# Expert blocks that skip empty places, and scan outputs made one head at a time

## The chip, the core and the metric

One Trainium2 chip, one of its cores. The metric is device time in microseconds from the first to the last instruction of one execution. The engines are TensorE (PE in the rows, its weight load PEld), VectorE (DVE), ScalarE (ACT), GpSimd (POOL) and SyncE (SP), which only issues DMAs here. 16 DMA engines move the data between HBM and SBUF for all of them.

## The reference

Two layers over 768 tokens of width 1024: 256 of a context and 512 latent ones. Layer 0 works on all 768, layer 1 updates the 512 latent ones alone. A layer has two halves.

The token mixer projects the tokens and sends them through a gated convolution and, beside it, through a recurrent scan in two directions with 8 heads of 64 channels. With a state S of 64 x 64 for each head and direction, one step is

```
sa = S kk;   S = S * decay - sa b^T + v k^T;   y = S r
```

The mixture of experts chooses for each token one of 4 groups and 2 of its 8 experts, so that 2 of 32 experts work on each token:

```
for expert e:  yb = (silu(xb @ w1[e]) * (xb @ w3[e])) @ w2[e]      # xb: the tokens of e
out[token] = sum over its two experts of gate * yb[its place]
```

Layer 0 thus fills 768 x 2 = 1536 places, layer 1 512 x 2 = 1024. A final RMSNorm closes the trunk. All data are float32.

## The kernel before

The two layers run one after the other, and a layer has four stages: the dense input products with the preparation of the scan (`stage_dense`), the scan itself (`stage_scan`), the output products and the router (`stage_out`, `route`), and the experts with the combination of their rows (`moe`, `combine`). A planner orders the instructions of each engine by its own model of their costs. Where the code says `manual_schedule`, the named engines keep the order in which the code issues; TensorE does so from `stage_dense` through the scan.

**Scan.** The tokens are cut into 12 chunks of 64. Heads are taken two at a time, a pair filling 128 partitions, and two pairs with both directions go together (`a` = 0, 1). `step` is one chunk: it forms right-hand sides from the state, multiplies them with inverted triangular matrices, updates the state (`St`, a block diagonal matrix of 128 x 128 for a pair, one 64 x 64 block for each head) and then makes the outputs, lines 966 to 983. The outputs of a chunk go into one PSUM tile `py`. For each of the four (pair, direction) groups, line 972 multiplies the state with the queries, all 128 columns of the state at once. It is left out in the first chunk, whose state is zero. Line 974 then adds, for each head apart, the product of its values with the masked scores. Layer 1 makes outputs from chunk 4 on only. The masks and the inverses of the next six chunks are made ahead in `inverses`: a substitution of 31 pairs of VectorE operations (lines 840 and 842), transposes (844, 846), then products on TensorE (864 and 874). Dense products of the convolution and the gates (`fillers`, line 331) stand between the steps, a fixed number after each part of a step. Their weights come through `weights` (line 222: load `wr`, three buffers; lines 312 and 313 split it into two parts). A float32 product shows as two records in the profile.

**Zeroing.** `bufY` in HBM has a row for each place: 32 experts of 64 places (`CAP`), then 24 overflow blocks of 64. `zero_rows` (line 162) clears the overflow rows in 12 writes of 512 KB on SP, each the repetition of a zeroed tile of 128 columns. They are issued one after another by the fillers of layer 0; the planner moved them up to the start of the first dense stage.

**Experts.** `route_ordered` gives every token a place in each of its two experts, and makes `slot`: for each place the number of its token, by a product of one-hot matrices with the token numbers `tok` (lines 1283 to 1292). A place without a token gets 0. The filled places of an expert are its first ones. `block` (line 1379) handles one expert: `gather` (line 1372) fetches the 64 rows of its places from `h2rows` with an indirect DMA on GpSimd into `xe` (two buffers); TensorE transposes them (line 1387); the products with w1, w3 and w2 follow (line 1399), six loads of 1 MB a block from SP through rings of 16 buffers (`er`, `ez`, `ex`, line 1136); and line 1421 stores the 64 result rows to their rows of `bufY`, a plain DMA on GpSimd. A block holds 72 matmuls. An expert with more than 64 tokens has overflow blocks; layer 0 runs one of them always and more in a loop if needed, layer 1 only in the loop. In this run there are 33 blocks in layer 0 and 32 in layer 1. `combine` fetches for each token its two rows of `bufY` (line 1459) and sums them with the gates.

Of the kernel before, what the change touches and what calls it, by code (L numbers as in the profile page):

```python
# [12 lines left out]
I32 = mybir.dt.int32  # L13
# [35 lines left out]
NOV = 24  # L49
DEC = math.exp(-0.5) / 2.0  # L50
NEG = -1.0e30

W_IN_ORDER = ([24, 25, 26] + [b + p for p in range(4) for b in (12, 16, 20)]
              + [b + j for j in range(4) for b in (4, 8, 0)]
# [11 lines left out]
CO = {}  # L66
_o = 0
for _n, _w in (("ident", 128), ("mask", 128), ("bones", 128), ("bmean", 128), ("ones", 128), ("ii", 64), ("tri", 128),
               ("i64", 64), ("sel", 2), ("i8", 8), ("i4", 4), ("i24", 24), ("i64k", 12), ("tok", 6)):
    CO[_n] = slice(_o, _o + _w)  # L70
    _o += _w
NCO = _o
# [2 lines left out]
def constants():  # L75
    c = np.zeros((P, NCO), np.float32)
    p = np.arange(P)[:, None]
    q = np.arange(P)[None, :]
    c[:, CO["ident"]] = p == q
    s = p % C  # L80
    t = q % C
    c[:, CO["mask"]] = np.where(q < C, s < t, s <= t)
    c[:, CO["bones"]] = (p // 64) == (q // 64)
    c[:, CO["bmean"]] = ((p // 64) == (q // 64)) * (-1.0 / 64)
    c[:, CO["ones"]] = 1.0
    c[:, CO["ii"]] = (p % 64) == np.arange(64)[None, :]
    c[:, CO["tri"]] = p < q
    c[:, CO["sel"]] = (p % 32) == np.arange(2)[None, :]
    c[:, CO["i64"]] = np.arange(64)
    c[:, CO["tok"]] = p + P * np.arange(6)  # L90
    c[:, CO["i8"]] = np.arange(8)
    c[:, CO["i4"]] = np.arange(4)
    c[:, CO["i24"]] = np.arange(24)
    c[:, CO["i64k"]] = 64.0 * (1 + np.arange(12))
    m = np.zeros((P, T + 1024), np.float32)
    m[:, :T] = (np.arange(T) % C) != 0
    m[:, T:] = np.eye(32, dtype=np.float32).reshape(1, 1024)
    return c, m
# [16 lines left out]
class Trunk:  # L115
# [46 lines left out]
    def zero_rows(self, pool):  # L162

        nc = self.nc
        z = self.sb(pool, [P, 128], "zrow")
        nc.gpsimd.memset(z, 0.0)
        v = self.bufY[NE * CAP:].rearrange("(p r) d -> p (r d)", p=P)
        n = v.shape[1]
        for i in range(0, n, 1024):
            nc.sync.dma_start(v[:, i:i + 1024].rearrange("p (a d) -> p a d", d=128),  # L170
                              rap(z[:], 0, [[0, 8], [1, 128]]))
            yield


# [736 lines left out]
    def step(self, a, i, AMs, Rf, RR, VU, KTr, nxt):  # L911


        nc, sp, k = self.nc, self.sp, self.k
        hq = [slice(h * 64, h * 64 + 64) for h in range(2)]
        prs = range(2)
        AM, ui = AMs[i % H], 4 * (i % H)
        if i == 0:
            self.Yt[a] = self.sb(sp, [P, 2, T], "Y")
            for j in range(2):  # L920
                s = self.St[a, j] = self.sb(sp, [P, 2, 2, P], f"St{j}")
                nc.gpsimd.memset(s, 0.0)
        Y = self.Yt[a]
        S = self.St[a, i % 2]
        if 0 < i < NCK - 1:
            S0 = self.sb(sp, [P, 2, 2, C], "S0", bufs=2)
            for q in hq:
                nc.gpsimd.tensor_tensor(S0[q], S[q, :, :, q],
                                        self.PC[q, 2 * a:2 * a + 2, :, i - 1:i].to_broadcast([C, 2, 2, C]), op=ALU.mult)
        ps = self.psum("pc", [P, 2, P], 2)  # L930
        for pr in prs:
            for d in range(2):
                ur = slice(64 - 64 * d, 128 - 64 * d)
                if i:
                    nc.tensor.matmul(ps[ur, pr], RR[:, pr, d, :C], S[:, pr, d, :], start=True, stop=False)
            for h, q in enumerate(hq):
                for d in range(2):
                    ur = slice(64 - 64 * d, 128 - 64 * d)
                    nc.tensor.matmul(ps[ur, pr, q], AM[:, d, pr, h, :C], VU[:, d, pr, q], start=i == 0,
                                     stop=i == 0 or h == 1)  # L940
        W = self.sb(sp, [P, 2, P], "W")
        nc.scalar.activation(W, ps, AF.Copy)
        yield 2
        ps = self.psum("pc", [P, 2, P], 2)
        for pr in prs:
            for h, q in enumerate(hq):
                for d in range(2):
                    ur = slice(64 - 64 * d, 128 - 64 * d)
                    nc.tensor.matmul(ps[ur, pr, q], Rf[ur, ui + 2 * pr + h, :], W[ur, pr, q], start=True, stop=True)
        nc.vector.tensor_copy(VU[64:128, 0], ps[64:128])  # L950
        nc.scalar.activation(VU[0:64, 1], ps[0:64], AF.Copy)
        yield 2
        if i < NCK - 1:
            ps = self.psum("pc", [P, 2, 2, C], 2)
            for pr in prs:
                for d in range(2):
                    for h, q in enumerate(hq):
                        nc.tensor.matmul(ps[q, pr, d, :], KTr[:, pr, d, q], VU[:, d, pr, q], start=True, stop=True)
            Sn = self.St[a, (i + 1) % 2]
            for q in hq:  # L960
                if i:
                    nc.vector.tensor_tensor(Sn[q, :, :, q], ps[q], S0[q], op=ALU.add)
                else:
                    nc.vector.tensor_copy(Sn[q, :, :, q], ps[q])
            yield 1
        yield from nxt
        if i >= self.c0:
            ps = self.psum("py", [P, 2, 2, C])
            for pr in prs:
                for d in range(2):  # L970
                    if i:
                        nc.tensor.matmul(ps[:, pr, d, :], S[:, pr, d, :], RR[:, pr, d, C:], start=True, stop=False)
                    for h, q in enumerate(hq):
                        nc.tensor.matmul(ps[q, pr, d, :], VU[:, d, pr, q], AM[:, d, pr, h, C:], start=i == 0, stop=True)

            m = CCK - 1 - i if i < CCK else NCK - 1 + CCK - i
            yf = Y[:, :, i * C:(i + 1) * C]
            yr = rap(Y[:], m * C + C - 1, [[T, 2], [-1, C]])
            for y, q in ((yf, ps[:, :, 0, :]), (yr, ps[:, :, 1, :])):
                if i < m:  # L980
                    nc.scalar.activation(y, q, AF.Copy)
                else:
                    nc.vector.tensor_tensor(y, y, q, op=ALU.add)
        yield 2
# [164 lines left out]
    def moe(self):  # L1149
# [5 lines left out]
        self.gathered = []  # L1155
        with tc.manual_schedule(engines={mybir.EngineType.Pool}):
            for e in range(2):
                self.gathered.append(self.gather(self.slot[:, e:e + 1]))
        self.prefetch(RING[l][2])
        for e in range(NE):  # L1160
            self.block(self.slot[:, e:e + 1], self.bufY[e * CAP:(e + 1) * CAP, :],
                       t["w1"][l, e], t["w3"][l, e], t["w2"][l, e])
            if e == 0:
                self.route_rest()
        n = 1 if self.full else 0
        for i in range(n):
            e = nc.values_load(self.ovt[0:1, i:i + 1], engines=[mybir.EngineType.SP], min_val=0, max_val=NE - 1)
            self.block(self.slot_over[:, i:i + 1], self.bufY[(NE + i) * CAP:(NE + i + 1) * CAP, :],
                       *self.chosen(e))
        self.overflow(n)  # L1170
        self.bp.release()
        self.ep2.release()
# [33 lines left out]
    def route_ordered(self):  # L1206
# [82 lines left out]
        count = self.sb(mp, [P, NE], "count")  # L1289
        V.tensor_copy(count, ps[:, nt, :])  # L1290
        self.slot = self.sb(mp, [CAP, NE], "slot", I32)
        V.tensor_copy(self.slot, pt)
        self.places = count, pos, oh2, ex

    def route_rest(self):

# [55 lines left out]
        for i in range(2 * nt):  # L1352
            self.nc.tensor.matmul(ps, Q[:, i, :], B[:, i, :], start=i == 0, stop=i == 2 * nt - 1)
        self.slot_over = self.sb(mp, [CAP, NOV], "slotv", I32)
        V.tensor_copy(self.slot_over, ps)
        pg = s_([nt], "pg")
        V.reduce_sum(pg, self.gexp, axis=AX.X)
        V.reciprocal(pg, pg)
# [10 lines left out]
        V.tensor_scalar(self.ovt[:, :NOV], ove, float(NE - 1), None, op0=ALU.min)  # L1369
        V.tensor_scalar(self.ovt[:, NOV:], ic[:, NE - 1:NE], 1.0 if self.full else 0.0, None, op0=ALU.max)  # L1370

    def gather(self, slot):

        xe = self.sb(self.bp, [CAP, D], "xe", bufs=2)
        self.nc.gpsimd.indirect_dma_start(out=xe[:], out_offset=None, in_=self.h2[:],  # L1375
                                          in_offset=bass.IndirectOffsetOnAxis(ap=slot, axis=0))
        return xe

    def block(self, slot, ydst, w1, w3, w2):

# [35 lines left out]
        yo = self.sb(self.bp, [P, D], "yo", bufs=2)[:CAP, :]  # L1418
        nc.scalar.activation(yo, py[CAP:], AF.Copy)  # L1419
        nc.vector.tensor_tensor(yo, py[:CAP], yo, op=ALU.add)  # L1420
        nc.gpsimd.dma_start(ydst, yo)

    def chosen(self, e):
        t, l = self.t, self.l
# [2 lines left out]
    def overflow(self, n0):  # L1427
# [2 lines left out]
        n = nc.values_load(self.ovt[0:1, NOV:NOV + 1], min_val=n0, max_val=NOV)  # L1430
        with tc.For_i(n0, n, 1) as i:
            e = nc.values_load(self.ovt[0:1, bass.ds(i, 1)], engines=[mybir.EngineType.SP], min_val=0, max_val=NE - 1)
            r = i * CAP + NE * CAP
            slot = self.sb(self.mp, [CAP, 1], "slot1", I32, bufs=1)
            nc.sync.dma_start(slot, self.slot_over[:, bass.ds(i, 1)])
            self.block(slot[:], self.bufY[bass.ds(r, CAP), :], *self.chosen(e))

    def combine(self):

# [119 lines left out]
```

## Time and profile before

| | |
|---|---|
| runs, us | 2964.94, 2961.85, 2952.41; median 2961.85 |
| profiled execution, us | 2971.3; span of its instructions 2969.3 |
| mean granted TensorE clock in it | 0.929 of full |
| busy share of the span | TensorE 87%, VectorE 42%, ScalarE 28%, GpSimd 14% |
| DMA | 741.84 MB, 250 GB/s over the span |

The stages of the profiled execution follow from the starts of their instructions: the first scan from about 365 to 840 us, the experts of layer 0 from about 1000 to 1555 us, the second scan from about 1935 to 2255 us, the experts of layer 1 from about 2383 to 2925 us.

In the rows, an engine's busy time counts its instructions' spans; several can overlap. A window's row gives, for PE, PEld, DVE, ACT and POOL in this order, busy us and the number of instructions, then the granted clock as a share of full, the share of the DMA engines' time and what they moved. In a timeline, the brackets at the end hold the idle time before and what ended it.

### The profile page before, as it was taken

The page shows a single profiled execution, that of the slowest core. Times are in us where ns is not written, and L with a number is a line of the kernel's source. Part 1 is how long each engine was busy: PE and PEld are TensorE (multiplying, and loading weights), DVE is VectorE, ACT ScalarE, POOL GpSimd, SP SyncE. Part 2 cuts the span into 40 slices and gives each one's busy share as a digit, 9 for nine tenths or more (in the row PEclk, how much of TensorE's full clock was granted, in tenths as well). Part 3 has the DMA queues.
Part 4 walks back from the last instruction along what each step waited for, and adds up shares of the span by engine and source line. Part 5 has one row for each costly group of instructions (what it writes and reads, how often), then busy time and mean ns, then how long its engine had stood idle before and what let it go on. Part 6 is the DMA issues. An engine that isn't in the chain of part 4 may idle for free. (4 is left out here: it accounts for less than half of the span.)

```text
span 2969.3 us, 44287 instructions
## 1 busy us (share of the span) xinstructions
PE 2571.9 (87%) x17505; PEld 1677.7 (57%) x17505; DVE 1237.5 (42%) x2618; ACT 838.4 (28%) x1603; POOL 422.9 (14%) x554
## 2 busy tenths in 40 slices
PE   6998899999989699888887997898998779888886
PEld 4676677777778443333337774566666634333334
DVE  4686553736463411111115786546646421111113
ACT  4453333333222111111112552443442211111111
POOL 0232011111130200000001231111211110000001
PEclk9999899998989799999998998888999989999998
DMA  7457445552554899999974467554446699999994
GB/s 277 138 164 228 147 159 166 166 183 84 170 179 150 319 403 393 398 398 392 398 311 169 119 188 243 188 167 132 144 127 187 233 345 391 391 397 400 390 404 157
DMA packets 284833, 741.84 MB, mean 250 GB/s; under 512 B 53712, under 2 KB 138960, under 8 KB 228560
## 3 DMA queue, kind: packets, MB, share of 16 engines
q1 hardware_dynamic: 271344, 694.42, 65.1%
q0 software_dynamic: 13280, 44.57, 4.5%
q8 instruction: 139, 2.28, 0.3%
q14 instruction: 70, 0.57, 0.1%
HBM read 647.41 MB, written 91.49 MB: 249 GB/s over the span
## 5 line engine op out<-in xcount | busy, mean ns | idle before, releaser
L331 PE MATMUL pd<-hh,wh 128*128 128x512 f32 (+1 forms) x912 | 352.4, 426 | 11.7 <-ACT hh L312 3.8
L331 PE MATMUL pd<-hh,wl 128*128 128x512 f32 (+1 forms) x912 | 311.7, 382 | 10.3 <-DVE wl L313 10.3
L331 PE MATMUL pd<-hl,wh 128*128 128x512 f32 (+1 forms) x912 | 311.7, 382 | 1.1 <-DVE hl L313 1.1
L1399 PE MATMUL pd<-ez,xs 128*64 128x512 f32 x1024 | 257.4, 635 | 37.6 <-DMA ez<-in_w 27.0
L313 DVE TENSOR_TENSOR wl<-wr,wh 128x512 fp32r<-128x512 f32 x236 | 166.2, 705 | 245.0 <-ACT wh L312 244.0
L1408 DVE COPY hs<-pd 128x512 f32<-128x512 f32 x65 | 45.0, 692 | 525.1 <-PE pd L1399 525.1
L312 ACT ACTIVATE wh<-wr 128x512 fp32r<-128x512 f32 x236 | 148.6, 631 | 321.3 <-PE pd L331 217.1
L331 PEld LDWEIGHTS pd<-hh,wh 128*128 128x128 f32 x912 | 163.5, 197 | 92.6 <-issue 30.1
L1399 PE MATMUL pd<-er,xs 128*64 128x512 f32 x672 | 172.9, 635 | 22.8 <-DMA er<-in_w 15.0
L331 PEld LDWEIGHTS pd<-hh,wl 128*128 128x128 f32 x912 | 163.7, 198 | 46.7 <-DVE wl L313 13.6
L1412 PEld LDWEIGHTS pt<-cst,hs 128*128 128x128 f32 x1040 | 125.6, 192 | 111.8 <-issue 56.0
L1420 DVE TENSOR_TENSOR yo<-py,yo 64x1024 f32<-64x1024 f32 x65 | 79.1, 1217 | 252.4 <-ACT yo L1419 239.4
L331 PEld LDWEIGHTS pd<-hl,wh 128*128 128x128 f32 x912 | 164.5, 198 | 29.5 <-DVE hl L313 2.3
L1399 PEld LDWEIGHTS pd<-ez,xs 128*64 128x64 f32 x1024 | 78.2, 144 | 178.2 <-issue 127.3
L1412 PE MATMUL pt<-cst,hs 128*128 128x64 f32 x1040 | 142.2, 281 | 26.5 <-DVE hs L1408 17.3
L1375 POOL DMA_INDIRECT xe<-h2rows,slot x64 | 60.0, 937 | 624.0 <-PE px L1387 595.4
L1399 PE MATMUL py<-ez,hid 128*64 128x512 f32 x520 | 127.7, 627 | 8.7 <-DVE yo L1420 7.8
L1389 ACT ACTIVATE xs<-px 128x512 f32<-128x512 f32 x65 | 38.8, 598 | 293.4 <-PE px L1387 287.6
L1399 PE MATMUL pd<-ex,xs 128*64 128x512 f32 x384 | 99.9, 644 | 21.7 <-DMA ex<-in_w 16.7
L1414 ACT ACTIVATE hid<-pt 128x256 f32<-128x256 f32 x65 | 25.0, 384 | 327.9 <-PE pt L1412 325.8
L1399 PEld LDWEIGHTS pd<-er,xs 128*64 128x64 f32 x672 | 48.9, 143 | 112.9 <-issue 83.6
L1410 ACT ACTIVATE hs<-pd 128x512 f32<-128x512 f32 x65 | 38.8, 597 | 240.9 <-PE pd L1399 240.8
(378 smaller groups left out, 4539.7 us busy)
## 6 DMA issues: line engine op xcount, KB each, us to landing
ez<-in_w SPq DMA_DIRECT2D x193, 1024.0 KB, 22.2
er<-in_w SPq DMA_DIRECT2D x125, 1024.0 KB, 22.3
ex<-in_w SPq DMA_DIRECT2D x72, 1024.0 KB, 22.3
wm<-in_w_mod SPq DMA_DIRECT2D x48, 1024.0 KB, 6.4
wr<-in_w_in SPq DMA_DIRECT2D x172, 256.0 KB, 3.1
bufY<-yo POOLq DMA_DIRECT2D x65, 256.0 KB
dKB<-KB SPq DMA_DIRECT2D x16, 768.0 KB, 5.2
dRR<-RR SPq DMA_DIRECT2D x16, 768.0 KB, 4.6
```

What stands on the lines that cost most here:

```text
L312: self.nc.scalar.activation(hi, src, AF.Copy)
L313: self.nc.vector.tensor_tensor(lo, src, hi, op=ALU.subtract)
L331: nc.tensor.matmul(p, a[:, k], h[:, kt, s], start=kt == 0 and j == 0, stop=kt == nk - 1 and j == 2)
L1375: self.nc.gpsimd.indirect_dma_start(out=xe[:], out_offset=None, in_=self.h2[:], in_offset=bass.IndirectOffsetOnAxis(ap=slot, axis=0))
L1389: nc.scalar.activation(xs, ps, AF.Copy)
L1399: nc.tensor.matmul(out[h * CAP:(h + 1) * CAP, c:c + 512], a[:, kt, :], w[:, i + h, c:c + 512], start=kt < 2, stop=kt >= nk - 2)
L1408: nc.vector.tensor_copy(hs, ps)
L1410: nc.scalar.activation(hs, ps, AF.Copy)
L1412: nc.tensor.matmul(pt[:, i, c, :], hs[:, c * P:(c + 1) * P], k["ii"], start=True, stop=True)
L1414: nc.scalar.activation(hid, pt[:, 0], AF.Silu)
L1420: nc.vector.tensor_tensor(yo, py[:CAP], yo, op=ALU.add)
```

## The change

Four edits go together.

Places without a token: `tok` holds the token number less `FAR` = 8192, and 8192 is added again when `slot` is made. A filled place has its token as before; an empty one has 8192. The gather gets a bound of 767 and drops places above it. The two buffers of `xe` are cleared before their first use.

Stores: `rows_of` makes `dst`, the row of `bufY` of each place, with 8192 added where the place is empty. The plain store becomes an indirect one over the whole of `bufY`, with its last row as the bound. The loop over further overflow blocks fetches its column of `dst` too.

Zeroing: `zero_rows` clears all 3584 rows instead of the 1536 of the overflow, in 28 writes of 512 KB, from a tile of 256 columns.

Scan outputs: the product with the state is made for each head apart, with the 64 columns of that head.

```diff
-    c[:, CO["tok"]] = p + P * np.arange(6)
+    c[:, CO["tok"]] = p + P * np.arange(6) - FAR
+    c[:, CO["row"]] = p + CAP * np.arange(NE + NOV)
...
-        z = self.sb(pool, [P, 128], "zrow")
+        z = self.sb(pool, [P, 256], "zrow")
         nc.gpsimd.memset(z, 0.0)
-        v = self.bufY[NE * CAP:].rearrange("(p r) d -> p (r d)", p=P)
+        v = self.bufY[:].rearrange("(p r) d -> p (r d)", p=P)
         n = v.shape[1]
         for i in range(0, n, 1024):
-            nc.sync.dma_start(v[:, i:i + 1024].rearrange("p (a d) -> p a d", d=128),
-                              rap(z[:], 0, [[0, 8], [1, 128]]))
+            nc.sync.dma_start(v[:, i:i + 1024].rearrange("p (a d) -> p a d", d=256),
+                              rap(z[:], 0, [[0, 4], [1, 256]]))
...
-                        nc.tensor.matmul(ps[:, pr, d, :], S[:, pr, d, :], RR[:, pr, d, C:], start=True, stop=False)
+                        for q in hq:
+                            nc.tensor.matmul(ps[q, pr, d, :], S[:, pr, d, q], RR[:, pr, d, C:], start=True, stop=False)
...
-                self.gathered.append(self.gather(self.slot[:, e:e + 1]))
+                self.gathered.append(self.gather(self.slot[:, e:e + 1], True))
...
-            self.block(self.slot[:, e:e + 1], self.bufY[e * CAP:(e + 1) * CAP, :],
+            self.block(self.slot[:, e:e + 1], lambda: self.dst[:, e:e + 1],
...
-        V.tensor_copy(self.slot, pt)
+        V.tensor_scalar(self.slot, pt, float(FAR), None, op0=ALU.add)
+        self.dst = self.sb(mp, [CAP, NE + NOV], "dst", I32)
+        self.rows_of(0, NE, self.slot)
...
+    def rows_of(self, a, b, slot):
+        V = self.nc.vector
+        V.tensor_scalar(self.dst[:, a:b], slot, float(FAR), float(FAR), op0=ALU.is_ge, op1=ALU.mult)
+        V.tensor_tensor(self.dst[:, a:b], self.dst[:, a:b], self.k["row"][:CAP, a:b], op=ALU.add)
...
-        V.tensor_copy(self.slot_over, ps)
+        V.tensor_scalar(self.slot_over, ps, float(FAR), None, op0=ALU.add)
+        self.rows_of(NE, NE + NOV, self.slot_over)
...
-    def gather(self, slot):
+    def gather(self, slot, first=False):
         xe = self.sb(self.bp, [CAP, D], "xe", bufs=2)
+        if first:
+            self.nc.gpsimd.memset(xe, 0.0)
         self.nc.gpsimd.indirect_dma_start(out=xe[:], out_offset=None, in_=self.h2[:],
-                                          in_offset=bass.IndirectOffsetOnAxis(ap=slot, axis=0))
+                                          in_offset=bass.IndirectOffsetOnAxis(ap=slot, axis=0),
+                                          bounds_check=T - 1, oob_is_err=False)
...
-        nc.gpsimd.dma_start(ydst, yo)
+        nc.gpsimd.indirect_dma_start(out=self.bufY[:], out_offset=bass.IndirectOffsetOnAxis(ap=dst(), axis=0), in_=yo,
+                                     in_offset=None, bounds_check=(NE + NOV) * CAP - 1, oob_is_err=False)
```

## Rows read from the trace of the kernel before

**Rows 1.** the page, share of DMA by slice, and its software queue

```profile
DMA  7457445552554899999974467554446699999994
q0 software_dynamic: 13280, 44.57, 4.5%
```

**Rows 2.** windows, experts of layer 1; columns: busy us (count) by engine, clock, DMA share, GB/s

```profile
2460.00:2520.00 60.00, 58.46 (x304) 25.06 (x302) 9.13 (x12) 9.80 (x15) 4.96 (x7) 1.00 1.02 391
```

**Rows 3.** waits of SP, experts of layer 0; columns: total us, times, longest

```profile
SPq L1136 <- DMA ez<-in_w: 164.4, 66, 4.2
```

**Rows 4.** windows over the two scans

```profile
365.00:840.00 475.00, 440.51 (x4264) 348.55 (x4263) 237.81 (x628) 151.27 (x343) 74.32 (x126) 0.95 0.50 157
1935.00:2255.00 320.00, 291.81 (x2947) 215.53 (x2945) 180.65 (x455) 118.69 (x265) 54.91 (x93) 0.93 0.47 143
```

**Rows 5.** DMA queues, 1100 to 1500 us; columns: packets, MB, share of 16 engines

```profile
q1 hardware_dynamic: 20050, 146.03, 92.1%
```

**Rows 6.** a window in which GpSimd issues nothing

```profile
1490.00:1500.00 10.00, 9.21 (x46) 3.92 (x42) 0.69 (x1) 0.00 (x0) 0.00 (x0) 1.00 1.02 422
```

**Rows 7.** GpSimd's groups; columns: busy us, mean ns, idle before

```profile
L1375 POOL DMA_INDIRECT xe<-h2rows,slot x64 | 60.0, 937 | 624.0 <-PE px L1387 595.4 <-DMA h2rows<-hr 9.2 <-DMA xe<-h2rows,slot 7.7
...
L1421 POOL DMA_DIRECT2D bufY<-yo x65 | 34.8, 535 | 375.2 <-DVE yo L1420 349.4 <-DVEq L1431 25.8
...
L922 POOL MEMSET St<- 128x512 f32 x8 | 4.1, 525 | 31.4 <-PE py L972 26.2 <-issue 5.3
```

**Rows 8.** waits of GpSimd, experts of layer 0

```profile
POOL xe L1375 <- PE px L1387: 263.5, 23, 16.9
```

**Rows 9.** timeline of GpSimd, start of the experts; columns: start us, us

```profile
999.18 1.14 POOL L1375 DMA_INDIRECT xe<-h2rows,slot  x1 [3.99 <-DVE slot L1292]
```

**Rows 10.** timeline of TensorE, one output block of the scan

```profile
509.94 0.33 PE L972 MATMUL py<-RRs,St 128*128 128x64 f32 x2
510.20 0.34 PE L974 MATMUL py<-AM,VU 128*64 128x64 f32 x4
...
512.35 0.49 PE L250 MATMUL pd<-cst,mrow 128*128 128x2 f32 x3
```

**Rows 11.** timeline of TensorE, the first chunk's output block

```profile
368.97 0.69 PE L974 MATMUL py<-AM,VU 128*64 128x64 f32 x16
369.59 0.62 PE L331 MATMUL pd<-hh,wh 128*128 128x512 f32 x2
```

**Rows 12.** the product with S, whole run; columns: ns min/median/max, first and last start

```profile
L972 PE MATMUL py<-RRs,St x304: 217/275/476, 381.8 to 2246.2; 128*128 128x64 f32 x152
...
L974 PE MATMUL py<-AM,VU x640: 222/270/369, 369.0 to 2246.5; 128*64 128x64 f32 x160
```

**Rows 13.** VectorE's groups, the substitution

```profile
L840 DVE TENSOR_TENSOR tmp<-AlTc,Tl 128x31 f32<-128x31 f32 (+15 forms) x248 | 90.8, 366 | 5.6
```

**Rows 14.** waits of TensorE in the scan of layer 0

```profile
PE pA L864 <- DVE AlTc L846: 1.7, 2, 1.1
```

**Rows 15.** timeline of SP while bufY is zeroed

```profile
57.42 10.79 SPq L170 DMA_DIRECT2D bufY<-zrow  x7
68.31 1.53 SPq L222 DMA_DIRECT2D wr<-in_w_in  x1
69.88 7.70 SPq L170 DMA_DIRECT2D bufY<-zrow  x5
77.68 29.54 SPq L222 DMA_DIRECT2D wr<-in_w_in  x7
```

**Rows 16.** timeline of TensorE behind the zeroing

```profile
84.54 0.80 PE L331 MATMUL pd<-hh,wh 128*128 128x512 f32 x1 [3.14 <-ACT wh L312]
```

**Rows 17.** windows while and after bufY is zeroed

```profile
60.00:65.00 5.00, 5.00 (x31) 4.34 (x30) 0.85 (x2) 2.08 (x4) 0.00 (x0) 1.00 1.11 340
85.00:90.00 5.00, 5.00 (x11) 2.68 (x11) 1.22 (x3) 1.95 (x4) 0.00 (x0) 0.50 0.30 105
90.00:95.00 5.00, 5.00 (x14) 3.52 (x14) 1.76 (x1) 0.20 (x1) 2.15 (x1) 0.54 0.01 3
```

More of the change, by code (lines that the diff above doesn't have):

```diff
@@ L51 @@
 NEG = -1.0e30
+FAR = 8192
 W_IN_ORDER = ([24, 25, 26] + [b + p for p in range(4) for b in (12, 16, 20)]
@@ L68 @@
 for _n, _w in (("ident", 128), ("mask", 128), ("bones", 128), ("bmean", 128), ("ones", 128), ("ii", 64), ("tri", 128),
-               ("i64", 64), ("sel", 2), ("i8", 8), ("i4", 4), ("i24", 24), ("i64k", 12), ("tok", 6)):
+               ("i64", 64), ("sel", 2), ("i8", 8), ("i4", 4), ("i24", 24), ("i64k", 12), ("tok", 6), ("row", NE + NOV)):
     CO[_n] = slice(_o, _o + _w)
@@ L1167, in moe @@
             e = nc.values_load(self.ovt[0:1, i:i + 1], engines=[mybir.EngineType.SP], min_val=0, max_val=NE - 1)
-            self.block(self.slot_over[:, i:i + 1], self.bufY[(NE + i) * CAP:(NE + i + 1) * CAP, :],
-                       *self.chosen(e))
+            self.block(self.slot_over[:, i:i + 1], lambda: self.dst[:, NE + i:NE + i + 1], *self.chosen(e))
         self.overflow(n)
@@ L1370, in route_rest, with block @@
         V.tensor_scalar(self.ovt[:, NOV:], ic[:, NE - 1:NE], 1.0 if self.full else 0.0, None, op0=ALU.max)
-    def gather(self, slot):
+    def gather(self, slot, first=False):
         xe = self.sb(self.bp, [CAP, D], "xe", bufs=2)
+        if first:
+            self.nc.gpsimd.memset(xe, 0.0)
         self.nc.gpsimd.indirect_dma_start(out=xe[:], out_offset=None, in_=self.h2[:],
-                                          in_offset=bass.IndirectOffsetOnAxis(ap=slot, axis=0))
+                                          in_offset=bass.IndirectOffsetOnAxis(ap=slot, axis=0),
+                                          bounds_check=T - 1, oob_is_err=False)
         return xe
-    def block(self, slot, ydst, w1, w3, w2):
+    def block(self, slot, dst, w1, w3, w2):
         nc, k = self.nc, self.k
@@ L1432, in overflow @@
             e = nc.values_load(self.ovt[0:1, bass.ds(i, 1)], engines=[mybir.EngineType.SP], min_val=0, max_val=NE - 1)
-            r = i * CAP + NE * CAP
             slot = self.sb(self.mp, [CAP, 1], "slot1", I32, bufs=1)
             nc.sync.dma_start(slot, self.slot_over[:, bass.ds(i, 1)])
-            self.block(slot[:], self.bufY[bass.ds(r, CAP), :], *self.chosen(e))
+            dst = self.sb(self.mp, [CAP, 1], "dst1", I32, bufs=1)
+            nc.sync.dma_start(dst, self.dst[:, bass.ds(NE + i, 1)])
+            self.block(slot[:], lambda: dst[:], *self.chosen(e))
     def combine(self):
```

## The prediction

> **What bounds the kernel now.** I read the slices of the page first, then windows over the stretches that the change touches, then the waits inside them. The DMA slices [rows 1] show two plateaus of nines: these are the two expert stages. A 60 us window in the second has the DMA engines full (share 1.02) while TensorE is busy 58.46 of 60 us [rows 2]. SP there waits for its own earlier loads to land before it may issue the next (66 times for the tag ez alone in 400 us) [rows 3]. So an expert stage ends when its bytes have been moved. TensorE's own pace is faster: that window has 304 matmuls, 72 make a block, so a block takes it 60/304 x 72 = 14.2 us. The scan stages are the opposite: TensorE is busy 440.51 of 475 us and 291.81 of 320 us [rows 4], DMA about half. There a TensorE instruction less is time less, as long as no other engine's chain takes its place. The chain of waits covers only the last 48 us (the final combine) and says nothing on these stages.
>
> **Expert stage: what a place costs.** In the 400 us from 1100 to 1500, 146.03 MB of weights arrived [rows 5], 365.1 GB/s. A block needs six loads of 1.0486 MB, 6.291 MB: 17.23 us. Where GpSimd issued nothing for 10 us, the engines moved 422 GB/s [rows 6], and 6.291 MB would take 14.91 us. The difference, 2.32 us a block, is what one gather and one store (64 rows of 4 KB each, 0.524 MB together) cost the weights. By bytes alone at 422 GB/s they would cost 1.24 us.
>
> **How many places are empty.** Each token goes to two experts: 1536 filled places in layer 0 and 1024 in layer 1. The 65 stores [rows 7] are 33 blocks and 32 blocks of 64 places, 2112 and 2048. So 576 and 1024 places are empty, together 1600, or 25 whole blocks' worth of gather and store. If a skipped place costs nothing and frees all that it costs now: 25 x 2.32 = 58 us. By bytes: 25 x 1.24 = 31 us. If a skipped row is still walked at full price, or relieves only transfers that nobody waits for: 0. I take 31, halfway between the ends. No row shows how a skipped row is treated. The DMA stays the bound: even at full relief a block of layer 1 falls by 1.16 to 16.1 us, still above 14.2.
>
> The Trainium skill says in SBUF — State Buffer, on the DMA port swizzle, that a tile on partitions 0 to 63 reaches only half of the ports. By that rule a gather holds back the weights for longer than its bytes, and the trace agrees (2.32 against 1.24 us). By it, too, the relief is uneven, since the empty places are always the last of a block; that is rival 2, and with it the experts' term would be between -17 and 0 instead of -31.
>
> **GpSimd.** The store becomes an indirect DMA: 0.94 us of issue in place of 0.54 [rows 7], 65 times 0.4. Before a gather GpSimd waits 263.5/23 = 11.5 us for TensorE [rows 8], so this is hidden; without that cover it would be 26 us. All stores now name the whole of bufY, so each waits for the landing of the one before, issued some 17 us earlier; queued behind it is the next gather, with the same 11.5 us of room. Only the last store of each stage is in the open: +0.8 us. The two clears of xe lie on GpSimd ahead of the first two gathers; 1024 elements at the pace of the 512-element clear (0.525 us) [rows 7] are about 1 us (an estimate). GpSimd idles 3.99 us before the first gather [rows 9], which hides the first; the second delays a gather that a whole block covers. The added VectorE operations, two per call on at most 64x32, are small, and VectorE is idle most of the stage: 0.
>
> **Scan outputs.** Now each of the four (pair, direction) groups of an output block issues one product with all 128 columns of S, then two of 64 columns. One starts at 509.94 and the next line follows at 512.35: 2.41 us [rows 10]. The first such product starts 0.26 us before the 64-column ones; every change of width costs. A block of the very first chunk has no product with S and runs 16 records of 64 columns in 0.62 us [rows 11]. All 16 end after 0.69 us and the shortest takes 0.22 [rows 12], so 15 starts take 0.47 us, 31 ns each: the two halves run beside each other. The new block is 32 such records: 0.62 + 16 x 0.031 = 1.11 us, 1.30 us less. The 304 records of that line [rows 12], 8 a block, are 38 blocks (22 in layer 0, 16 in layer 1): 49 us of TensorE. Bounds: 0, if all of it turns to waiting, and 50.
>
> Some of it will. VectorE's substitution runs 31 pairs of operations of 0.37 us [rows 13], about 23 us, beside three to four steps, and TensorE already waits for its end twice in layer 0 [rows 14]. 9 of the 22 output blocks and 8 of the 16 lie beside that chain: 17 x 1.30 = 22 us at risk. I count half as lost, 11 us: 38 us remain. What is late next is this transposed result at L864.
>
> The Trainium skill speaks against this edit: TensorEngine Tiling (Array Packing), section Instruction Overhead, says that each matmul carries about 60 cycles of overhead, so that cutting an already small one in two gains nothing. By that page the 304 records added would cost 8 us more at 2.4 GHz (an estimate), and the scan's term would be -30 instead of -38. The 31 ns between starts are measured on such small records and contain whatever they cost, so the sum stays.
>
> **Zeroing.** The diff zeroes all 3584 rows of bufY: 28 writes of 512 KB in place of 12. SP issues them early and in one queue with the weights of the first dense products. The 12 hold SP for 10.79 + 7.70 us, 1.54 us each, and the load between them is issued at 68.31, the next at 77.68 [rows 15]. TensorE then runs dry and waits 3.14 us [rows 16], after which the granted clock is 0.50 of full, the lower level of 1.2 GHz [rows 17]. A load feeds 24 matmuls, and 31 pass in 5 us [rows 17], 3.9 us. If 16 more writes follow in the same pattern, seven to a load, they take 16 x 1.54 = 24.6 us and let through 2.3 loads, 9 us of work: 15 us lost. Bounds: 0, if they fall into idle stretches of the queue, and 25, fully serial. I take 15, since the twelve already starve TensorE.
>
> **Sum.** -31 - 38 + 15 + 1 = -53 us on the profiled execution, 2971.3 to 2918. That execution is 9.4 us above the median of the runs, 2961.85; from the median I forecast 2909 us.
>
> **Rivals.**
> 1. *Full relief.* A skipped place frees all of its 36 ns: -58 in place of -31, 2882 us. For it: the gap of 1.08 us between cost and bytes has to belong to the same 128 rows. Against it: only if the rows left are spread evenly.
> 2. *Little relief.* The filled places are always the first of a block, so the early partitions keep their traffic. If each engine serves partitions of its own and a weight load waits for the slowest engine, then of the 2.32 us only what the late partitions take away goes: half of the 1.08 us above the bytes in layer 1, 0.54 x 32 = 17 us at most, and nearly nothing in layer 0; or nothing, if skipped rows are still walked. Experts -17 to 0, the whole 2923 to 2940 us. The Trainium skill's section on the port swizzle (SBUF — State Buffer) would lead here.
> 3. *VectorE keeps the scan.* TensorE's gain beside the substitution is lost entirely, and part of the rest to the reductions of the read-out: -20 in place of -38, 2927 us. For it: TensorE waits at L864 already. Against it: only 34 of 475 us of the first scan are TensorE idle [rows 4].
> 4. *The clock falls in the scan* (the slower side). Today short idle there is rare, and the scan of layer 0 runs at 0.95 of full clock [rows 4]. After the wait of 3.14 us [rows 16] the clock was at half for about 10 us [rows 17], which costs 5 us. If shorter output blocks open such a gap in the steps, each costs 5: from 11 of the 38 steps on (11 x 5 = 55) the whole gain is gone, and with every second step, 19 x 5 = 95, it is 2909 + 95 = 3004 us. Against it: the dense products that fill the scan stay where they are.
>
> **Chances.** Forecast 0.45 (its own range 2890 to 2925), full relief 0.18, little relief 0.20, VectorE 0.10, clock 0.05, the rest for something unnamed. The range takes in rivals 1 to 3 and most of the bounds of the zeroing: 2862 to 2945. What can be told from no change is about 0.5%, 15 us: faster means under 2947. Forecast and rivals 1 to 3 all lie there, though the slow end of rival 2 with 10 us more of zeroing does not: faster 0.87, same 0.08, slower 0.05.
>
> **What would show it.** *Experts:* the stretch from first gather to last store shortens by about 12 us in layer 0 and 19 us in layer 1, and the software queue's bytes over the run fall from 44.57 MB [rows 1] by 13.1 MB; unchanged bytes or unchanged stretches mean rival 2. *Scan:* output blocks of 32 records in 1.1 us; idle at L864 grows by no more than 11 us; a granted clock well under 0.95 is rival 4. *Zeroing:* 28 writes on SP before about 100 us, and TensorE dry for some 15 us more. The prediction is wrong if the weights' rate in the expert stages does not rise above 365 GB/s, or if the new output blocks take more than 2 us.

## The result and the profile after

The changed kernel takes 2937.2 us (median of 19 runs, 2924.8 to 2946.1), the kernel before 2958.0 beside it (19 runs): a ratio of 0.9927 [0.9912, 0.9942], 21 us faster where 53 were forecast. 2937 lies in the range, far from 2909. The profiled execution went from 2969.3 to 2935.9 us of span.

The stages, from the starts of their instructions in each trace. A scan runs from its first product on `RRi` to its last read-out, an expert stage from `slot` to the first gather of the combination. "Last load" is when the last weight load of the stage leaves SyncE, counted from the stage's start. The kernels below the first two are those of the experiments.

| kernel | ahead of scan 0 | scan 0 | experts 0 (last load) | scan 1 | experts 1 (last load) | span |
|---|---|---|---|---|---|---|
| before | 268.2 | 560.3 | 560.8 (523.9) | 465.6 | 546.7 (508.8) | 2969.3 |
| the change | 280.5 | 536.2 | 568.0 (534.2) | 446.3 | 533.3 (501.2) | 2935.9 |
| e1_scan_only | 265.2 | 533.1 | 560.2 (523.0) | 450.2 | 549.9 (509.7) | 2927.3 |
| e2_gather_skip_plain_store | 272.8 | 534.1 | 546.3 (505.2) | 450.6 | 522.3 (485.5) | 2895.9 |
| e5_list_store_all_rows | 266.8 | 534.8 | 573.9 (542.6) | 447.6 | 563.0 (530.4) | 2958.1 |
| e6_change_no_skip | 279.2 | 535.4 | 574.9 (540.4) | 450.9 | 561.2 (528.6) | 2966.5 |
| b1_bunched_list | 266.9 | 536.6 | 553.6 (519.4) | 453.5 | 546.5 (512.1) | 2928.4 |
| c1_change_use_order | 279.6 | 536.2 | 544.4 (511.4) | 446.7 | 516.5 (482.5) | 2894.7 |

The scans gained 24 and 19 us and the stretch ahead of scan 0, where the zeroing lies, cost 12, near the forecast. The experts gained 13 in layer 1 and lost 7 in layer 0, where 19 and 12 less were forecast (from first gather to last store, as the prediction put it: 16.4 less and 5.6 more).

The scans of the changed kernel by windows answer to [rows 4]: 13.6 and 13.7 us less TensorE in the same stretches, although 310 and 155 more of its records fall into them, at clocks of 0.95 and 0.92.

```profile
365.00:840.00 475.00, 426.90 (x4574) 340.10 (x4573) 245.58 (x643) 158.37 (x359) 80.63 (x136) 0.95 0.51 164
1935.00:2255.00 320.00, 278.09 (x3102) 206.84 (x3095) 185.94 (x467) 121.81 (x270) 63.42 (x107) 0.92 0.49 155
```

TensorE's wait for the substitution in that first stretch, 1.7 us in [rows 14], is 2.8 us (total us, times, longest); over the whole of the two scans it went from 12.4 to 13.5 and from 17.7 to 22.2 us. So 6 us of the gain turned into this wait, where the prediction allowed 11.

```profile
PE pA L866 <- DVE AlTc L848: 2.8, 1, 2.8
```

One new output block in TensorE's timeline (start, us): 32 records from 504.88, the next line at 505.96, 1.08 us where [rows 10] had 2.41.

```profile
504.88 0.34 PE L975 MATMUL py<-RRs,St 128*64 128x64 f32 x4
505.04 0.29 PE L977 MATMUL py<-AM,VU 128*64 128x64 f32 x4
...
505.74 0.29 PE L977 MATMUL py<-AM,VU 128*64 128x64 f32 x4
505.96 0.62 PE L333 MATMUL pd<-hh,wh 128*128 128x512 f32 x2
```

SyncE's timeline while `bufY` is zeroed answers to [rows 15]: 28 writes, seven to a load, the last issued at 99.6 us instead of 77.6.

```profile
57.54 8.84 SPq L172 DMA_DIRECT2D bufY<-zrow  x7
66.47 1.24 SPq L224 DMA_DIRECT2D wr<-in_w_in  x1
67.76 9.31 SPq L172 DMA_DIRECT2D bufY<-zrow  x7
...
89.76 9.80 SPq L172 DMA_DIRECT2D bufY<-zrow  x7
```

Windows over 57 to 115 us, before and after the change, show what this does to TensorE: 4.8 us less busy, at a granted clock of 0.80 instead of 0.91, and 58 fewer records.

```profile
57.00:115.00 58.00, 54.86 (x268) 43.00 (x267) 24.42 (x41) 23.68 (x47) 7.03 (x4) 0.91 0.60 178
57.00:115.00 58.00, 50.09 (x210) 37.74 (x208) 19.95 (x35) 19.37 (x36) 4.29 (x2) 0.80 0.89 297
```

The page's software queue (packets, MB, share) shows that the rows are skipped, 31.48 MB against 44.57 [rows 1]. But between 1100 and 1500 us the weights' queue (packets, MB, share) did not move more than in [rows 5], and one window of 25 us has the DMA engines at a share of 0.85 (last two columns: DMA share, GB/s).

```profile
q0 software_dynamic: 13280, 31.48, 3.3%
```

```profile
q1 hardware_dynamic: 19952, 145.29, 91.9%
```

```profile
1300.00:1325.00 25.00, 19.67 (x92) 7.53 (x93) 3.09 (x4) 3.58 (x6) 2.79 (x4) 0.86 0.85 323
```

The reason is in SyncE's waits of the same stretch (total us, times, longest): the weight loads wait most for TensorE to free a buffer, where [rows 3] had them wait for the landing of earlier loads.

```profile
SPq L1139 <- PE pd L1413: 141.2, 70, 8.3
SPq L1139 <- DMA ez<-in_w: 65.8, 26, 7.1
SPq L1139 <- PE py L1413: 65.2, 34, 6.2
```

GpSimd's groups over the whole run answer to [rows 7]: the store's issue costs 0.92 us, near the 0.94 of the forecast, and stores wait 107.9 us for the store before to land.

```profile
L1388 POOL DMA_INDIRECT xe<-h2rows,slot x64 | 60.9, 951 | 635.8 <-PE px L1401 616.9 <-DMA h2rows<-hr 8.5 <-issue 3.7
L1435 POOL DMA_INDIRECT bufY<-yo,dst x65 | 59.9, 921 | 329.2 <-DVE yo L1434 191.3 <-DMA bufY<-yo,dst 107.9 <-DVEq L1446 14.3
```

### The profile page after: what moved, and what is told of

The parts are those of the page before. It is cut to its first block, busy times and chain, and to the rows that moved or that the text cites. A ratio compares the mean times of both kernels' runs of the same rounds, so it can differ in the third digit from the quotient of the medians.

```text
span 2935.9 us, 44964 instructions
## 1 busy us (share of the span) xinstructions
PE 2526.1 (86%) x17809; PEld 1657.8 (56%) x17809; DVE 1237.9 (42%) x2626; ACT 837.2 (29%) x1603; POOL 451.2 (15%) x558
## 3 DMA queue, kind: packets, MB, share of 16 engines
q0 software_dynamic: 13280, 31.48, 3.3%
## 5 line engine op out<-in xcount | busy, mean ns | idle before, releaser
L1413 PE MATMUL pd<-ex,xs 128*64 128x512 f32 x384 | 111.6, 666 | 30.8 <-DMA ex<-in_w 30.8
L1429 DVE TENSOR_TENSOR hid<-hid,pt 128x256 f32<-128x256 f32 x65 | 27.2, 418 | 234.5 <-ACT hid L1428 233.8
L1433 ACT ACTIVATE yo<-py 64x1024 f32<-64x1024 f32 x65 | 66.4, 1021 | 179.6 <-PE py L1413 152.3
## 6 DMA issues: line engine op xcount, KB each, us to landing
er<-in_w SPq DMA_DIRECT2D x125, 1024.0 KB, 15.4
ex<-in_w SPq DMA_DIRECT2D x72, 1024.0 KB, 13.1
```

The lines of the kernel that those rows point to most:

```text
L1413: nc.tensor.matmul(out[h * CAP:(h + 1) * CAP, c:c + 512], a[:, kt, :], w[:, i + h, c:c + 512], start=kt < 2, stop=kt >= nk - 2)
```

## The experiments

### Parts of the change, ordered by the planner

**e1_scan_only** is the kernel before with the hunk at line 972 alone.

> The kernel before with the scan's output blocks a head at a time and nothing else of the change. Two theories. ORDER: the stores by list all name the whole of bufY, so the planner bunches gathers, stores and products, the expert stages idle in turns and the freed traffic is lost. NO RELIEF: empty places hardly held the weight stream up, so skipping them frees little, in any order. Both say the same of this kernel: the pair of traces gave 24 us in scan 0 and 19 us in scan 1, so 43 us under the kernel before (35 to 47), and some 20 us faster than the kernel of the change.

2930.7 us, ratio 0.9920 [0.9890, 0.9949] to before: 24 us less, not 43. Its trace shows the full gain (scans 27.2 and 15.4 us shorter; of the other stages only the experts of layer 1 are longer, by 3.2).

**e2_gather_skip_plain_store**: in the changed kernel

```diff
-        nc.gpsimd.indirect_dma_start(out=self.bufY[:], ...
+        nc.gpsimd.dma_start(ydst, yo)
-        v = self.bufY[:].rearrange("(p r) d -> p (r d)", p=P)
+        v = self.bufY[NE * CAP:].rearrange("(p r) d -> p (r d)", p=P)
```

> The kernel of the change with the plain store of a whole block put back and only the 12 zero writes of before: scan by heads plus the skipping gather. Against e1_scan_only. ORDER: the gathers' half of the freed 13.1 MB counts at once, 16 us under e1 (10 to 22), because the stores don't name the whole of bufY and gathers and stores take turns again. NO RELIEF: within 5 us of e1.

2895.9 us, ratio 0.9800 [0.9774, 0.9827]: 35 us under e1, more than the whole forecast for the experts, with half of the skipping. Between 1100 and 1500 us the weights' queue moves

```profile
q1 hardware_dynamic: 20648, 150.34, 92.5%
```

375.9 GB/s, instead of 365.1 in the kernel before and 365.9 in e1. The theory of no relief falls.

**e5_list_store_all_rows** takes the plain store of e1 out and nothing is skipped. (It also keeps the change's gather with its bound, the two clears and the making of `dst`.)

```diff
-        nc.gpsimd.dma_start(ydst, yo)
+        nc.gpsimd.indirect_dma_start(out=self.bufY[:], out_offset=... dst() ...
```

> Scan by heads, stores by list, but every place is gathered and every row stored (empty places gather token 0), and 12 zero writes: the traffic of before in the order of the change. Against e1_scan_only. ORDER: 20 to 30 us slower than e1. NO RELIEF: 5 to 10 us slower (what is left of the difference between the kernel of the change and e1 after 12 us for the zeroing).

2958.9 us, ratio 1.0010 [0.9990, 1.0030]: 28 us over e1, in both expert stages (13.7 and 13.1 us). Stores by list, without any skipping, undo the whole gain of e1.

**e6_change_no_skip**: the changed kernel, where `FAR` is neither taken off `tok` nor added to `slot`.

> The kernel of the change, the same instructions in the same order, with the lists made so that no place is skipped in gather or store (empty places gather token 0): against the kernel of the change it tells what skipping itself is worth, against e5_list_store_all_rows what 16 more zero writes cost (12 us from the traces). ORDER: 25 to 31 us slower than the change. NO RELIEF: 0 to 8 us slower than the change.

2969.1 us, ratio 1.0050 [1.0028, 1.0071]: 32 us over the change, 10 over e5. So the change is, by medians: scan -24, stores by list +28, 16 zero writes +10, skipping -32; the sum of -18 leaves 3 of the 21 us unassigned.

### The same in an even order, written by hand

In e1 the planner lets gather and store alternate on GpSimd through most of a stage. In e5, e6 and the change it does not: gathers often come in pairs, stores in runs of up to four, and of seven to eleven at the end, and TensorE's products shift likewise. Four kernels fix one even order for both engines; their weight loads, too, are then issued in the order in which TensorE uses them:

```diff
+        with tc.manual_schedule(engines={E.PE, E.Pool}):
+            for e in range(1, NE + n):    # block e
+                # w1(e); transposes(e+1); gather(e+2); w3(e); w2(e-1), store(e-1)
```

**h0_hand_plain** is e1 in this order.

> e1_scan_only (all places gathered, plain stores, 12 zero writes) with the order of the expert blocks on TensorE and GpSimd written out by hand: products of w1, turning of the next block's rows, gather of the one after it, products of w3, w2 of the block before and its store. What is open is the 28 us by which stores by list made e1_scan_only slower in e5_list_store_all_rows. ORDER: the planner's bunched order costs them. LANDING: each store by list waits on GpSimd for the landing of the one before it, and holds the gathers behind it, in any order. Of this kernel both say: within 10 us of e1's 2931 (2920 to 2940); it is the base for the three that follow.

2932.5 us, ratio 0.9915 [0.9884, 0.9946]: as expected.

**h2_hand_gather_skip** adds the change's gather with its `slot`, as e2 did to e1.

> h0_hand_plain with the skipping gather alone (plain stores, 12 zero writes). Both theories: as in the planner's order, 35 us under h0 (25 to 40).

2899.0 us, ratio 0.9805 [0.9772, 0.9837]: 33.5 us under h0.

**h3_hand_list_no_skip** is e6 in this order, with this edit against the change:

```diff
-        V.tensor_scalar(self.slot, pt, float(FAR), None, op0=ALU.add)
+        V.tensor_scalar(self.slot, pt, 0.0, None, op0=ALU.add)
```

> h0_hand_plain with the stores by list and the 28 zero writes of the change, but no place skipped in gather or store (empty places gather token 0): the traffic of h0 and the zeroing. ORDER: only the 16 more zero writes are left, 10 us over h0 (5 to 14). LANDING: 38 us over h0 (30 to 45).

2953.1 us, ratio 0.9985 [0.9967, 1.0004]: 20.6 us over h0, between the two (in their two traces 10). Between 1100 and 1500 us its GpSimd has no wait for a landing; all that the stores wait for is their data:

```profile
POOL bufY L1506 <- DVE yo L1505: 348.3, 24, 15.9
POOL xe L1415 <- issue: 7.0, 23, 0.3
...
```

**h1_hand_change** is the whole change in this order.

> The whole change (skipping gather, stores by list that skip, 28 zero writes, scan by heads) in the order by hand. Against h3_hand_list_no_skip both theories say 32 us less, as between e6_change_no_skip and the change. ORDER: so 22 us under h0 and 28 us under the change (2905 to 2915). LANDING: within 8 us of the change's 2937.

2915.4 us, ratio 0.9862 [0.9830, 0.9894]: 22 us under the change, and 38 under h3. An even order thus takes away most of the 28 us; which property of it does so, these four don't tell, since the loads' order changed with it.

### Four controls

**before_again** is the kernel before, unchanged, for a second trace.

> The kernel before once more, for its trace: the traces of six kernels with the scan by heads all show 532 to 536 us from the first state product to the last read-out in scan 0 and 446 to 451 us in scan 1, against 560 and 466 us in the one trace of the kernel before, 42 us in all, while the medians of e1_scan_only give 24 us. If that one trace was a long execution, this one shows some 550 and 460 us, 25 us in all; if the scan does gain 42 us, it shows 560 and 466 again and e1_scan_only loses the rest elsewhere.

The two scans take 558.8 and 466.4 us, in an execution of 2967.7 us. So a profiled execution shows 42 us of gain in the scans, while the medians of e1's and before's runs lie 24 apart. Both profiled executions of the kernel before were 10 us and more above the median of its runs beside them (2957), e1's (2929.3) was not. Where the timed runs spend their time isn't recorded; this stays open.

**h4_hand_list_store_all_rows** is h1 with the 12 zero writes of before and

```diff
-        V.tensor_scalar(self.dst[:, a:b], slot, float(FAR), float(FAR), op0=ALU.is_ge, op1=ALU.mult)
+        V.tensor_scalar(self.dst[:, a:b], slot, float(FAR), 0.0, op0=ALU.is_ge, op1=ALU.mult)
```

> h2_hand_gather_skip with the stores by list, that store every row (no row skipped), and 12 zero writes. What is open: h3_hand_list_no_skip stood 21 us over h0_hand_plain by the medians, 10 us of it for the zeroing; in the traces the two expert stages were only 1.5 us longer each. ORDER ALONE: in an even order the store by list costs nothing, within 4 us of h2 (2895 to 2903). LIST: the list itself costs the other 10 us, 2905 to 2914.

2908.1 us, ratio 0.9826 [0.9810, 0.9842]: 9 us over h2. The list itself does cost some 9 us even in an even order, 7.5 of them in the experts of layer 0 by the traces (556.4 against 548.9). Against h1 (7 us more, with 16 more zero writes) the skipped stores are worth only some 3 us, if the 16 writes cost here the 10 us that they cost between e5 and e6; the two expert stages together are 4.7 us shorter in h1's trace.

**z1** and **z2** move the zero writes, by source tiles that depend on the gates:

```diff
-        nc.gpsimd.memset(z, 0.0)
+                nc.gpsimd.tensor_scalar(z, src[0][:, :256], 0.0, None, op0=ALU.mult)    # src: tg, a gate
```

> h1_hand_change with its 28 zero writes tied to the gates' tiles, two writes behind each of 14 tiles, so that they leave SyncE at the end of the projections and in scan 0 and not at 57 to 100 us. PLACE: the writes cost by holding the weight loads' queue and engines where the weights bound the time; later they cost nothing: 28 / 16 of 10 us, 17 us under h1 (2895 to 2902). BYTES: 14.7 MB cost the same wherever they are written: within 5 us of h1's 2915.

2900.8 us, ratio 0.9798 [0.9781, 0.9816]: 14.6 under h1. The 28 writes now leave SyncE at 437 to 693 us:

```profile
L173 SPq DMA_DIRECT2D bufY<-zrow x28: 370/498/1427, 437.5 to 692.5; - x28
```

> h2_hand_gather_skip with its 12 zero writes moved in the same way, one behind each of 12 gate tiles. PLACE: 12 / 16 of 10 us, 7 us under h2 (2889 to 2895). BYTES: within 3 us of h2's 2899.

2895.7 us, ratio 0.9784 [0.9765, 0.9804]: 3.3 under h2, half of what was expected, and the runs of the two overlap (2889.5 to 2899.1 and 2892.0 to 2903.4). In both traces the stretch ahead of scan 0 falls (by 20.1 and 7.6 us) and scan 0 itself grows (by 7.8 and 5.2): place decides, but later isn't free.

### The order of the weight buffers

`expert_weights` gives each load the next buffer of a ring of 16 (5 `er`, 8 `ez`, 3 `ex`) in the order in which the code issues the blocks. The planner then orders TensorE and the loads as it likes. Two kernels replay the order of e5 unit by unit (a turning, a product, a store), so that the code issues the loads in the order in which TensorE uses them:

```diff
+SEQ = ("GGxGxGddxGtxGtYxGSdddtdtddYSttddYtt...", ...)    # d: w1 or w3, Y: w2, S: store
+            for c in SEQ[l]:
+                emit(c)
```

**b1_bunched_list** keeps the stores by list.

> e5_list_store_all_rows with its own order of TensorE and GpSimd in the expert blocks written down block by block and replayed, so that now the weight loads, too, follow the order in which TensorE uses them (in e5 they take their buffers in the order of the blocks and leave SyncE in the planner's order). Control for b0_bunched_plain. If the bunched order of TensorE and GpSimd, with or without the waits for landings, costs the 18 us that an even order saved: 2959 again (2952 to 2966). If it was the order of the weight buffers: near the 2942 of an even order with list stores (h4_hand_list_store_all_rows's 9 us over plain stores, put on h0_hand_plain's 2932).

2920.0 us, ratio 0.9858 [0.9828, 0.9889]: 39 us under e5, with the same order of units on TensorE and of gathers and stores on GpSimd. (One difference is left: in e5 the planner splits some units and puts other work between their parts, in b1 each unit is whole. What this is worth was not tried apart.) The theories of the runs by hand, order and landing, both said 2959; the buffers' order, put at 2942, was worth 22 us more than that. First SyncE's waits in e5, 1100 to 1500 us, then those of b1:

```profile
SPq L1139 <- DMA ez<-in_w: 101.1, 41, 8.0
SPq L1139 <- PE pd L1413: 80.9, 44, 3.7
...
SPq L1139 <- PE py L1413: 48.1, 24, 5.2
```

```profile
SPq L1141 <- DMA ez<-in_w: 175.0, 71, 5.1
...
SPq L1141 <- PE pd L1507: 1.0, 3, 0.5
SPq L1141 <- PE py L1507: 1.0, 4, 0.3
```

129 us of waiting for TensorE became 2. The issues show it too (start, us), e5 first and then b1, 1130 to 1200 us: short runs with holes between them, up to 7.5 us, against whole turns of the ring.

```profile
1136.60 0.33 SPq L1139 DMA_DIRECT2D ez<-in_w  x1
1139.05 0.33 SPq L1139 DMA_DIRECT2D ex<-in_w  x1
1144.64 0.33 SPq L1139 DMA_DIRECT2D er<-in_w  x1
1146.36 0.33 SPq L1139 DMA_DIRECT2D ez<-in_w  x1
1154.17 4.24 SPq L1139 DMA_DIRECT2D ex<-in_w  x2
```

```profile
1131.96 21.34 SPq L1141 DMA_DIRECT2D ez<-in_w  x7
1157.11 5.71 SPq L1141 DMA_DIRECT2D ex<-in_w  x3
1165.48 10.41 SPq L1141 DMA_DIRECT2D er<-in_w  x5
1178.06 21.44 SPq L1141 DMA_DIRECT2D ez<-in_w  x8
```

The holes of this stretch did not cost e5 its time. From 1100 to 1500 us the weights' queue moved almost as much in e5 as in e1 (e1 first) and in b1 (146.60 MB):

```profile
q1 hardware_dynamic: 20100, 146.36, 92.2%
q1 hardware_dynamic: 20002, 145.65, 91.9%
```

Layer 0 loses its time at the end of the stage. Counted from the stage's start, the 191st of its 198 weight loads leaves SyncE at 501.5 us in e5 and at 503.1 in e1, the last one at 542.6 and 523.0. Between them lies e5's longest hole, 20.5 us without a load, in which SyncE waits 14.4 us for one product of TensorE (total us, times, longest) and then 5.9 us for a landing:

```profile
1489.52 0.34 SPq L1139 DMA_DIRECT2D ex<-in_w  x1
1510.33 3.78 SPq L1139 DMA_DIRECT2D er<-in_w  x2
```

```profile
SPq L1139 <- PE pd L1413: 14.4, 1, 14.4
```

In layer 1 the lag builds up over the stage: 13.0 us at the 181st of 192 loads, 20.7 at the last. After the first 40 us of each stage, e5 has 18 gaps of more than 6 us between two loads; e1 and b1 have none. TensorE's granted clock over the stage of layer 0 goes with this: 0.94 in e1, 0.91 in e5 and in the change, 0.95 in b1. Whether the lower clock adds to the time of its own was not separated.

The waits for landings, on the other hand, are still there in b1, as in e5 (first e5, then b1):

```profile
POOL bufY L1435 <- DMA bufY<-yo,dst: 73.6, 9, 10.1
```

```profile
POOL bufY L1206 <- DMA bufY<-yo,dst: 56.6, 8, 8.9
```

**b0_bunched_plain** has plain stores in the same order.

> b1_bunched_list with plain stores, which wait for no other store's landing, in the same order of TensorE and the same order of gathers and stores on GpSimd. ORDER: bunching alone costs, so it stays within 10 us of b1 (what the list itself costs), about 2949. WAITS: the cost is that a store holds GpSimd and the gathers behind it until the store before it has landed, which bunched stores run into; without that it comes down to the 2931 of e1_scan_only and h0_hand_plain.

2915.6 us, ratio 0.9843 [0.9813, 0.9874]: 4 us under b1, 15 under e1. So bunched work costs nothing here, and the list with its waits for landings at most these 4 us. The rest of what e5 lost came back with the loads in the order of use. The loads of e1 are bound in the order of the blocks too, and there SyncE waited only 3 us for TensorE from 1100 to 1500 us, so it is this binding together with e5's order that costs. Why b0 also beats e1 and h0 (17 us) wasn't followed up.

**c1_change_use_order** is the whole change on top of b1.

> The whole change (skipping gather, skipping stores by list, 28 early zero writes, scan by heads) with the replayed bunched order and the weight loads in the order of their use, as in b1_bunched_list. If the order of the weight buffers was the cost of the stores by list, it is the change less the 39 us between e5 and b1: 2898 (2890 to 2908), as far under the kernel before as the prediction wanted (its 2909, and 7 us more). If b1 owes its gain to something that the full traffic alone shows, 2915 (h1_hand_change) or more.

2896.9 us, ratio 0.9805 [0.9774, 0.9835]: the change with its loads in the order of use stands 40 us below the change, where expected. That is 54 us under the kernel before beside it, like the 53 of the forecast, but partly by luck: the order of the loads, which is no part of the change, gives some 15 us even with plain stores (e1 to b0). The weights in 1100 to 1500 us:

```profile
q1 hardware_dynamic: 20638, 150.29, 94.1%
```

375.7 GB/s, after 363.2 in the change.

**c0_plain_use_order** is b0 with h2's gather and z2's zero writes.

> The best parts together: b0_bunched_plain (plain stores, weight loads in the order of use) with the skipping gather (-35, as e2 against e1 and h2 against h0) and the 12 zero writes in the scan (-3, as z2 against h2): 2878 (2872 to 2886). If the gather's relief and that of the weight buffers are the same idle time of the weight queue, it stays at e2's and z2's 2896.

2869.9 us, ratio 0.9712 [0.9680, 0.9743], 2 us below the expected range: the reliefs add. This version, with plain stores, is 81 us faster than the kernel before beside it (2950.5) and 67 under the change's median.

## Why the prediction was wrong

**The step that failed** is that of GpSimd, "All stores now name the whole of bufY, so each waits for the landing of the one before", with its price: hidden, and "only the last store of each stage is in the open: +0.8 us". The end of a stage did come out like that (from the last w2 product to the combination 7.5 us in e5, 6.3 in e1). But the stores by list cost 28 us elsewhere. I took the order of the work from the trace of before as given, and asked only what waits in it. With stores by list the planner made another order for TensorE and for the loads; that their common target is the reason is likely, but was not tried apart from the other ways in which such a store differs. SyncE's queue then stood before buffers that TensorE freed late: the last load left 19.6 and 20.7 us later in e5 than in e1, and b1, with the loads in the order of use, takes 3.6 us less than e1 for the one and 2.4 more for the other. No rival had it. The condition that I had put under "wrong" is what the trace shows: the weights' rate, 363 GB/s, did not rise above 365.

**Experts, -31.** As the worth of skipping this held: -32 (e6 to the change), -38 (h3 to h1), -35 and -33.5 for the gather alone. That is near the value by bytes and well short of -58, so rival 1 is out. That the number came out is partly luck: I priced gather and store alike, but nearly all comes from the gather, at more than twice the price by its bytes, and the store gave almost nothing.

**Rival 2, little relief**, gave a time near the result (2923 to 2940) for a reason that is false. The Trainium skill's rule on the port swizzle (SBUF — State Buffer) stood behind it; the traces disagree with what I drew from it, since the late partitions' rows, left out of the gather alone, freed 14.7 us in layer 0 and 20.3 in layer 1 (h0 to h2), more than rival 2 allowed for gather and store together (nearly nothing and 17).

**Scan, -38.** Output blocks of 1.08 us (1.11 forecast); the scans shorter by 24.1 and 19.3 us in the trace of the change, 24 us in all by the medians of e1. By the medians that is 14 us less than forecast, and rival 3's 20 is nearer. The traces speak against rival 3: the wait for the substitution grew by 6 us in both scans together, the wait for the read-out's operand `yr` by some 7 in the first (5.9 to 12.6 us). Why the medians show less than the traces is open. By the section Instruction Overhead of the Trainium skill (TensorEngine Tiling (Array Packing)) a block would have been some 0.2 us longer than my sum (an estimate); the measured block is shorter than the sum.

**Zeroing, +15.** +10 by e5 and e6, +12.4 ahead of scan 0 in their traces. It is the place of the writes that costs, as z1 shows; whether through the queue or through the time of the DMA engines (share 0.89 instead of 0.60 in the windows above) is not separated. The sign that I named did not come: TensorE ran dry for 5 us more, not 15, and the rest goes with its lower clock. **The clock** (rival 4) did not fall in the first scan, and by 0.01 in the second.

In sum, by the medians: the stores took 27 us more than forecast, the scan gave 14 less, the zeroing took 5 less and the skipping gave 1 more. That is 35 us, for a gain of 21 instead of 53; 3 us stay unassigned. The stores are by far the largest of these terms, and the one whose mechanism the prediction lacked.

## What to carry to other kernels

When an edit changes what an instruction depends on, a planner may reorder its neighbours; the cost of the wait itself then says little. Where loads rotate through a ring of buffers, let the ring turn in the order of use: look at whether the load queue waits for landings (good) or for the engine that frees buffers, and above all at the last loads of a stage, behind which nothing is left to catch up. And skip the rows of a gather before those of a store, if the second needs clearing and a common target.

## What the runs showed of the hardware that was not expected

Here a gathered row weighed far more on the weight stream than a stored one. The empty places take 6.5 MB out of the gathers and as much out of the stores; the first gave 34 us (e1 to e2, h0 to h2), more than the 15.5 us that 6.5 MB take at the 422 GB/s of [rows 6], the second some 3 us (h4 to h1). Why is open; the packets in the traces don't name their DMA engine. One rival is untested: in the kernels that skip nothing, all empty places fetch the same row, that of token 0, and a list of different rows was not tried.

A skipped row isn't free of packets: the changed kernel's software queue still has 13280, as in [rows 1], with fewer bytes. In the trace's packet records 3200 of them have shrunk from 4096 to 4 bytes; packets of 4 bytes took 11 ns on average there, those of 4096 bytes 197.
